# A decoder step on one core: where the recurrence's small products and the square sums stand among the large projections

## The chip, the cores and the metric

The kernel runs on one core of a Trainium2 chip. A core has five engines with their own instruction streams: PE multiplies matrices, DVE, ACT and POOL work on vectors, and SP issues DMA transfers (the others can issue some too). They meet at semaphores. The metric is the device time of one launch in microseconds (us).

## The reference

One inference step of a decoder with two layers of width 1024 in float32. A prompt of 16 + 1024 tokens and eight single sample tokens go through a causal convolution layer, an MLP, an RWKV-7 layer, a second MLP and a final norm. The change lies in the RWKV-7 layer, whose core is this (cut):

```python
r = (xr @ w_r).astype(f32)
k = (xk @ w_k).astype(f32)
v = (xv @ w_v).astype(f32)
w_log = -jax.nn.softplus(-(w0 + jnp.tanh(xw @ w1) @ w2).astype(f32)) - 0.5
decay = jnp.exp(-jnp.exp(w_log))
a = jax.nn.sigmoid((a0 + (xa @ a1) @ a2).astype(f32))
g = jax.nn.sigmoid(xg @ g1) @ g2
...
kk = (k * k_k.astype(f32)).reshape(hs)
kk = kk / jnp.maximum(jnp.sqrt(jnp.sum(kk * kk, axis=-1, keepdims=True)), L2_EPS)
...
def _wkv7_step(S, inp):
    r_t, w_t, k_t, v_t, kk_t, a_t = inp
    sa = jnp.einsum('bhvk,bhk->bhv', S, -kk_t)
    S = (S * w_t[:, :, None, :] + sa[..., None] * (kk_t * a_t)[:, :, None, :]
         + v_t[..., None] * k_t[:, :, None, :])
    y = jnp.einsum('bhvk,bhk->bhv', S, r_t)
    return S, y
```

The three large projections have 1024 x 1024 weights; decay, a and g come through low-rank pairs of weights (64, 64 and 128 wide). The state S has 16 heads of 64 x 64 and runs over the prompt's tokens one after the other.

## The kernel before

Activations lie with the channel on the 128 partitions, in eight blocks of channels (KT = 8), and the tokens along the row.

**Token groups.** The RWKV projections run in four groups of 272, 256, 256 and 264 tokens, called 0 to 3 here as in the code (`mixer_in(g, ...)`, L967); the third group is g == 2. In a group the loop over p (L1108) takes one block of 128 output channels at a time: the projection pr with w_r (eight matmuls, `proj`, L919), perhaps a projection pk with w_k for the *next* group (`keys`, L927; `keys_amid` and `keys_behind` say which, L914), the low-rank products l_g, l_w and l_a (L1120, L1129), the projection pv with w_v (L1133). Then come the products of the block before (`finish`/`trace`, L1054): transposes vt, the small products nn, and the bonus sum (a matmul into a tile that is also called pk, L1101), and last pb, which spreads the norm of kk over its heads (L1141).

**The square sums.** `keys` needs the sum of the squares of k_k * k per head. ACT squares each pk into sq (L948), and four small matmuls add it into pn (L939). They stand one key block late: those of block p follow the projection of block p + 1.

**The recurrence** is computed in 17 chunks of 64 tokens. Its steps for a chunk are small products: A (L1274, on 64 rows), gg and po (L1325, 32 x 32), bT (L1343, full transposes), W (L1350), U (L1366), S (L1377) and Y (L1384, L1386). Between them DVE, ACT and POOL move results out of PSUM: w, uv, fs, sv, xa, nr, sw, no. DVE also inverts 32 x 32 triangles (L1236, L1237, tiles ni and tt), and finished rows are normed (ems, ey, eq on ACT and DVE, yn on PE). SP loads a chunk's operands (xa, bk, p, sv, uv) in between the blocks of weights.

**Ticks.** These steps are pushed into the projections by `tick` (L1584). Each call takes a step of the inversion, gives the recurrence some credit and lets it emit steps until the credit is used up, and takes a step of the norm:

```python
PACE = [0, 1.4, 1.3, 2.4]
...
def tick(g, slow):

    invert()
    advance(PACE[g] * slow, NCH - 1)
    next(ng, None)
```

Group 0 has pace 0, so its ticks emit nothing of the recurrence. A block p has five ticks: one at its start, two inside pr (after the third and the sixth matmul), two inside pv. A key projection has two of its own in groups 1 and 2 at the same two places (when it runs for the next group).

**What sets the order.** In this stage PE's instructions stand in the order in which the program writes them (`tc.manual_schedule(engines={nc.tensor.engine})`, L1590). The order on the other engines is chosen by a scheduler, when the program is built, from a timeline of its own. Results of matmuls go to PSUM: four banks (tag mm) rotate among the projections and low-rank products, three (tag w) among the recurrence's products, one (tag x) holds pn.

Of the kernel before, what the change touches and what calls it, by code (L numbers as in the profile page):

```python
# [8 lines left out]
F32 = mybir.dt.float32  # L9
# [7 lines left out]
P = 128  # L17
# [16 lines left out]
N1 = 272  # L34
# [12 lines left out]
def hybrid_step(tc, x_prompt, x_sample, state_conv, state_shift, state_wkv, meta_tokens,  # L47
# [10 lines left out]
    with ctx:  # L58
# [48 lines left out]
        for name, ap in vecs:  # L107
            n = ap.shape[0]
# [85 lines left out]
        def bank(name, tag="mm"):  # L194
            return cur[tag].tile([P, 512], F32, name=name, tag=tag)
# [200 lines left out]
        with ExitStack() as l0:  # L396
# [294 lines left out]
            with ExitStack() as s:  # L691
# [14 lines left out]
                for g in range(3):  # L706
# [125 lines left out]
        pr = pool(ld, "pr", 1)  # L832
# [85 lines left out]

        def proj(w, act, n, name, fill=None):  # L919
            ps = bank(f"p{name}")  # L920
            for k in range(KT):
                nc.tensor.matmul(ps[:, :n], w[:, k, :], act[k], start=k == 0, stop=k == KT - 1)  # L922
                if fill and k in (2, 5):
                    fill()
            return ps

        def keys(g, fill):  # L927
# [5 lines left out]
            pn = bank(nm("pn"), "x")  # L933
            add_pn = lambda: None

            def to_pn(p, sq):
                def add():
                    for j in range(4):
                        nc.tensor.matmul(pn[32 * j:32 * j + 32, :n // 4], head_sel(p), sq[:, n // 4 * j:n // 4 * (j + 1)],  # L939
                                         start=p == 0, stop=p == KT - 1, tile_position=(0, 32 * j))  # L940
                return add
            for p in range(KT):
                yield
                ps = proj(next(wrkv), act, n, nm("k", p), fill)
                k_ = kept[g, p] = pr.tile([P, N1], F32, name=nm("st", p), tag="st", bufs=KT + 1)
                nc.scalar.copy(k_[:, :n], ps[:, :n])
                sq = pr.tile([P, N1], F32, name=nm("sq", p), tag="rk", bufs=2)
                nc.scalar.activation(sq[:, :n], ps[:, :n], AF.Square, scale=vec("k_k", p))  # L948
                add_pn()
                add_pn = to_pn(p, sq)  # L950
            yield
# [3 lines left out]
            norm[g] = lorap.tile([P, N1], F32R, name=nm("r16"), tag="r16", bufs=2)[:, :n]  # L955
            add_pn()
            nc.vector.tensor_scalar(r16, pn[:, :w], L2_EPS * L2_EPS, None, op0=ALU.max)
# [9 lines left out]
        def mixer_in(g, tick):  # L967
# [63 lines left out]
            def t_(name, p, tag=None, bufs=1):  # L1031
                return pr.tile([P, N1], F32, name=nm(name, p), tag=tag or name, bufs=bufs)
# [8 lines left out]
            dd = lambda p, i, src: nc.gpsimd.tensor_copy(ddec[:, p, i, :], src)  # L1041
            both = lambda: tick(1.0)
            wg, ww = gate_w(), rate_w()
            gate(wg)
# [9 lines left out]
            def finish(p, rk, ab, vv):  # L1054
                def trace():
                    for s in segs:
# [41 lines left out]
                    if g == 0:  # L1098
                        nc.gpsimd.dma_start(d_n[0, p], n32[:, 4])
                    pb = bank(nm("pk", p))  # L1100
                    nc.tensor.matmul(pb[:, :n], hsum, rk[:, :n], start=True, stop=True)  # L1101
# [4 lines left out]

            late, later = (lambda: lambda: None), lambda: None
            for p in range(KT):  # L1108
                both()
                ps = proj(next(wrkv), act, n, nm("r", p), both if p else first)  # L1110
                rk2 = pr.tile([P, 2, N1], F32, name=nm("rk2", p), tag="rk2", bufs=2)
# [23 lines left out]
                nc.scalar.copy(vv[:, :n], ps[:, :n])  # L1135
                later()
                later = late()
                nkk, rp = (rk2[:, i, :] for i in range(2))
# [649 lines left out]
```

## Time and profile before

| | |
|---|---|
| median of three runs | 2652.7 us (2650.81 to 2654.59) |
| profiled execution | 2651.75 us |
| its span, first to last instruction | 2649.8 us |
| mean granted clock of PE | 0.994 |
| groups 0 to 3 of the projections, from about | 1106, 1236, 1396 and 1562 us |
| PE busy in the stretch from 1106 to 1713 us | 582.3 of 607 us |

The span is that of the profiled execution; times inside it are counted from its first instruction. In the rows of the instructions in order of time, a row holds a start, a busy time from the first start to the last end, the engine, the line, and the result and operands of a run of equal instructions; `128*128` is the part of PE's array that a matmul uses (rows times columns). One float32 matmul is recorded as two, so a projection of eight is x16. Behind them in brackets stands the idle time before a row and who ended it. In the rows by stretch, the columns are the stretch, its length, the busy time of each engine with its count of instructions, PE's granted clock, the share of the DMA engines and GB/s.

### The profile page before, as it was taken

The page shows a single profiled execution, that of the slowest core. Times are in us where ns is not written, and L with a number is a line of the kernel's source. Part 1 is how long each engine was busy: PE and PEld are TensorE (multiplying, and loading weights), DVE is VectorE, ACT ScalarE, POOL GpSimd, SP SyncE. Part 2 cuts the span into 40 slices and gives each one's busy share as a digit, 9 for nine tenths or more (in the row PEclk, how much of TensorE's full clock was granted, in tenths as well). Part 3 has the DMA queues.
Part 4 walks back from the last instruction along what each step waited for, and adds up shares of the span by engine and source line. Part 5 has one row for each costly group of instructions (what it writes and reads, how often), then busy time and mean ns, then how long its engine had stood idle before and what let it go on. Part 6 is the DMA issues. An engine that isn't in the chain of part 4 may idle for free.

```text
span 2649.8 us, 51719 instructions
## 1 busy us (share of the span) xinstructions
PE 2594.1 (98%) x19956; PEld 2432.9 (92%) x19956; DVE 1717.6 (65%) x3610; ACT 1128.8 (43%) x2093; POOL 1456.7 (55%) x2060
## 2 busy tenths in 40 slices
PE   9999999999999999999999999899999999999998
PEld 8999999999999999777777777789999999999998
DVE  6999999997444444445757567686679554444435
ACT  5546435444444333243344545545444542222223
POOL 7677878878878777022211113476588763333331
PEclk9999999999999999999999999999999999999999
DMA  7663544554446543677776867898575542222211
GB/s 190 172 168 108 167 141 133 160 172 137 138 138 187 155 136 112 191 211 202 214 184 181 213 160 194 218 207 195 142 219 174 153 132 65 72 68 69 72 48 44
DMA packets 602060, 400.24 MB, mean 151 GB/s; under 512 B 96128, under 2 KB 548928, under 8 KB 601814
## 3 DMA queue, kind: packets, MB, share of 16 engines
q1 hardware_dynamic: 573764, 360.08, 49.6%
q0 software_dynamic: 8720, 26.35, 3.0%
q10 hardware_dynamic: 19330, 10.49, 1.4%
q8 instruction: 158, 2.59, 0.4%
q14 instruction: 88, 0.72, 0.1%
HBM read 338.94 MB, written 58.83 MB: 150 GB/s over the span
## 4 chain that ended last, share of the span: by engine, by line
PE 85%; DVE 8%; ACT 2%; issue 2%; DMA 1%; POOL 1%; SPq 0%; ACTq 0%; DVEq 0%; POOLq 0%
PE ps_in L190 8%; PE ps_in L192 8%; PE ps_in L191 8%; PE out L190 8%; PE out L191 8%; PE out L192 8%; PE pk L922 4%; PE pr L922 4%; PE pv L922 3%; PE ps_g L190 1%; PE ps_o L192 1%; PE ps_g L191 1%; PE ps_g L192 1%; PE ps_oo L190 1%; PE ps_o L190 1%
## 5 line engine op out<-in xcount | busy, mean ns | idle before, releaser
L165 POOL TENSOR_TENSOR wo_lo<-wo_raw,wo_hi 128x256 fp32r<-128x256 f32 x736 | 543.0, 770 | 286.6 <-ACT wo_hi L158 279.2
L165 POOL TENSOR_TENSOR wi_lo<-wi_raw,wi_hi 128x256 fp32r<-128x256 f32 x640 | 474.5, 774 | 238.3 <-ACT wi_hi L158 237.9
L190 PE MATMUL out<-hh,wo_hi 128*128 128x352 f32 (+2 forms) x1536 | 497.5, 324 | 8.1 <-DVE h L360 6.5
L360 DVE TENSOR_TENSOR h<-h,out 128x352 f32<-128x352 f32 (+2 forms) x768 | 386.9, 512 | 168.2 <-PE out L192 166.6
L190 PE MATMUL ps_in<-m_h,wi_hi 128*128 128x352 f32 (+2 forms) x1536 | 494.0, 322 | 0.0
L192 PE MATMUL ps_in<-m_l,wi_hi 128*128 128x352 f32 (+2 forms) x1536 | 492.8, 321 | 0.7 <-DVE m_l L288 0.7
L191 PE MATMUL out<-hh,wo_lo 128*128 128x352 f32 (+2 forms) x1536 | 492.5, 321 | 0.0
L191 PE MATMUL ps_in<-m_h,wi_lo 128*128 128x352 f32 (+2 forms) x1536 | 491.5, 320 | 0.0
L192 PE MATMUL out<-hl,wo_hi 128*128 128x352 f32 (+2 forms) x1536 | 490.8, 320 | 0.0
L542 DVE SCALAR_TENSOR_TENSOR cv<-u,wdw,cv 128x348 f32<-128x348 f32 (+2 forms) x720 | 378.8, 577 | 0.7
L158 ACT CAST wi_hi<-wi_raw 128x1024 fp32r<-128x1024 f32 x160 | 167.6, 1049 | 383.7 <-PE out L192 191.1
L158 ACT CAST wo_hi<-wo_raw 128x1024 fp32r<-128x1024 f32 x184 | 192.7, 1048 | 313.0 <-PE out L192 167.1
L190 PEld LDWEIGHTS out<-hh,wo_hi 128*128 128x128 f32 x1536 | 289.1, 188 | 13.7 <-DVE h L360 9.0
L190 PEld LDWEIGHTS ps_in<-m_h,wi_hi 128*128 128x128 f32 x1536 | 289.2, 188 | 1.4
L192 PEld LDWEIGHTS ps_in<-m_l,wi_hi 128*128 128x128 f32 x1536 | 288.2, 188 | 2.0 <-DVE m_l L288 1.5
L191 PEld LDWEIGHTS out<-hh,wo_lo 128*128 128x128 f32 x1536 | 288.5, 188 | 0.8
L191 PEld LDWEIGHTS ps_in<-m_h,wi_lo 128*128 128x128 f32 x1536 | 288.5, 188 | 0.6
L192 PEld LDWEIGHTS out<-hl,wo_hi 128*128 128x128 f32 x1536 | 288.3, 188 | 0.0
L347 DVE SCALAR_TENSOR_TENSOR ps_in<-ps_in,rs_m 128x352 f32<-128x352 f32 (+2 forms) x192 | 100.7, 525 | 256.5 <-PE ps_in L192 256.1
L142 DVE TENSOR_TENSOR hl<-ps_in,hh 128x352 fp32r<-128x352 f32 (+2 forms) x192 | 98.9, 515 | 124.0 <-ACT hh L141 123.9
L1097 POOL DMA_DIRECT2D d_n<-n x32 | 24.5, 764 | 220.4 <-DVE n L1087 130.8
L348 ACT ACTIVATE ps_in<-ps_in 128x352 f32<-128x352 f32 (+2 forms) x192 | 85.1, 444 | 129.4 <-DVE ps_in L347 129.2
(371 smaller groups left out, 4734.5 us busy)
## 6 DMA issues: line engine op xcount, KB each, us to landing
wi_raw<-in_w_mlp_in_dram SPq DMA_DIRECT2D x160, 512.0 KB
wo_raw<-in_w_mlp_out_dram SPq DMA_DIRECT2D x160, 512.0 KB
wk_raw<-in_rwkv_w_k_dram SPq DMA_DIRECT2D x32, 512.0 KB
wr_raw<-in_rwkv_w_r_dram SPq DMA_DIRECT2D x32, 512.0 KB
wv_raw<-in_rwkv_w_v_dram SPq DMA_DIRECT2D x32, 512.0 KB
d_ab<-ab POOLq DMA_DIRECT2D x32, 512.0 KB, 4.3
pg_raw<-in_conv_w_pw_dram SPq DMA_DIRECT2D x24, 512.0 KB
pa_raw<-in_conv_w_pw_dram SPq DMA_DIRECT2D x24, 512.0 KB
```

The lines of the kernel that those rows point to most:

```text
L142: return eng_lo.tensor_sub(lo, src, hi.bitcast(F32))
L158: cast = nc.scalar.copy(hi[:, :a * b], raw[:, :a * b])
L165: eng_lo.tensor_sub(lo[:, cs], raw[:, cs], hi[:, cs].bitcast(F32))
L190: nc.tensor.matmul(ps, w[0], act[0], start=first, stop=False)
L191: nc.tensor.matmul(ps, w[1], act[0], start=False, stop=False)
L192: nc.tensor.matmul(ps, w[0], act[1], start=False, stop=last)
L347: nc.vector.scalar_tensor_tensor(s, s, 0.0, rs()[:, :n], op0=ALU.max, op1=ALU.mult)
L348: nc.scalar.activation(s, s, AF.Square)
L360: total = nc.vector.tensor_add(hv[:, 4 * i + m, :], hv[:, 4 * i + m, :], ps[:, :n])
L542: nc.vector.scalar_tensor_tensor(acc[m][:, :n], ug[:, m, j:j + n], wdw[:, m, j:j + 1], acc[m][:, :n], op0=ALU.mult, op1=ALU.add)
L922: nc.tensor.matmul(ps[:, :n], w[:, k, :], act[k], start=k == 0, stop=k == KT - 1)
L1097: nc.gpsimd.dma_start(d_n[ch0:ch0 + ncg, p].rearrange("c r t -> r c t"), n32[:, :ncg])
```

## The change

The ticks get other places. In groups 0, 1 and 3 a block still has five, one each: at the block's start (not for p = 0), in the middle of pr, behind l_w and l_a, in the middle of pv, and behind nn. In group 2 there are none in pr and pv (block 0 keeps two in pr, where the last step of the keys hangs on them): three follow each other behind l_w and l_a, and two behind nn. The ticks in the key projections stay.

The square sums are put on a list, `sums`, and emitted behind l_a of the block, each right after its own key projection rather than one later. sq and rk, which share a tag, get three buffers rather than two.

```diff
-        def proj(w, act, n, name, fill=None):
+        def proj(w, act, n, name, fill=None, at=(2, 5)):
             ps = bank(f"p{name}")
             for k in range(KT):
                 nc.tensor.matmul(ps[:, :n], w[:, k, :], act[k], start=k == 0, stop=k == KT - 1)
-                if fill and k in (2, 5):
+                if fill and k in at:
                     fill()
             return ps
+        sums = []
...
-            add_pn = lambda: None
-
...
-                sq = pr.tile([P, N1], F32, name=nm("sq", p), tag="rk", bufs=2)
+                while len(sums) > (p == 1 and g > 0):
+                    sums.pop(0)()
+                sq = pr.tile([P, N1], F32, name=nm("sq", p), tag="rk", bufs=3)
                 nc.scalar.activation(sq[:, :n], ps[:, :n], AF.Square, scale=vec("k_k", p))
-                add_pn()
-                add_pn = to_pn(p, sq)
+                sums.append(to_pn(p, sq))
...
-            add_pn()
+            sums.pop(0)()
...
+            lumps = g == 2
+            spaced = (lambda: None) if lumps else both
...
-                def trace():
+                def trace(fill):
...
+                    for _ in range(1 + lumps):
+                        fill()
                     pb = bank(nm("pk", p))
                     nc.tensor.matmul(pb[:, :n], hsum, rk[:, :n], start=True, stop=True)
...
             for p in range(KT):
-                both()
-                ps = proj(next(wrkv), act, n, nm("r", p), both if p else first)
+                if p:
+                    spaced()
+                ps = proj(next(wrkv), act, n, nm("r", p), *((spaced, (3,)) if p else (first,)))
...
+                while sums:
+                    sums.pop(0)()
+                for _ in range(3 if lumps and p else 1):
+                    both()
...
-                ps = proj(next(wrkv), act_v, n, nm("v", p), both)
+                ps = proj(next(wrkv), act_v, n, nm("v", p), spaced, (3,))
...
-                later = late()
+                later = late(both)
...
-                rk = t_("rk", p, "rk", 2)
+                rk = t_("rk", p, "rk", 3)
...
-                late()()
+                late(lambda: None)()
```

How this moves instructions is seen best in the order of single engines. First PE in block 4 of group 2, before (W, po and U are the recurrence's; the rows left out are matmuls of the same projection):

```order
L922 MATMUL pr_4_16361<-mx_0_5_15378,wr_4_raw 128x256
L1350 MATMUL W_16368<-sv,xa_12365 64x64 x16
L1325 MATMUL po_16390<-p_15917,gg_16280 32x32 x16
L922 MATMUL pr_4_16361<-mx_0_6_15380,wr_4_raw 128x256
...
L922 MATMUL pk_2_16415<-mx_2_7_15838,wk_2_raw 128x264
L939 MATMUL pn_15840<-sq_1_16237,hsel 32x66 x4
L1028 MATMUL l_g_16432<-lg_15328,wg_12353 128x256
L1129 MATMUL l_w_16438<-lwa,wa_12355 128x256
L1129 MATMUL l_a_16439<-lwa,wa_12355 128x256
...
L922 MATMUL pv_4_16448<-mx_3_2_15421,wv_4_raw 128x256
L1366 MATMUL U_16452<-w_16385,p_16283 64x64 x16
L922 MATMUL pv_4_16448<-mx_3_3_15423,wv_4_raw 128x256
```

and now:

```order
L922 MATMUL pk_2_16378<-mx_2_7_15838,wk_2_raw 128x264
L1028 MATMUL l_g_16391<-lg_15328,wg_12353 128x256
L1138 MATMUL l_w_16397<-lwa,wa_12355 128x256
L1138 MATMUL l_a_16398<-lwa,wa_12355 128x256
L938 MATMUL pn_15840<-sq_2_16389,hsel 32x66 x4
L1363 MATMUL W_16405<-sv,xa_12365 64x64 x16
L1338 MATMUL po_16427<-p_15931,gg_16319 32x32 x16
...
L922 MATMUL pv_4_16452<-mx_3_7_15431,wv_4_raw 128x256
L1070 MATMUL vt_3_16465<-ident,vv_3_16272 128x128 x2
L1087 MATMUL nn_3_16472<-ab_3_16360 32x32 x16
L1379 MATMUL U_16491<-w_16422,p_16322 64x64 x16
L1105 MATMUL pk_3_16520<-rk_3_16358,hsum 128x256
```

W, po and pn now follow l_a, pn with the sq of this block's own key (sq_2, not sq_1), U follows nn, and pr, pk and pv are whole.

Then ACT in block 1 of group 2, before (vv is the copy that empties pv; bkt, gg, p, ems are the recurrence's and the norm's):

```order
L1333 COPY gg_15719<-gg_15702 32x256 x2
L1146 ACTIVATE em_1_15793<-wa_1_15681 128x256
L1150 ACTIVATE ex_1_15795<-wa_1_15681 128x4x64
L1344 COPY bkt_15725<-bT_15726 128x512
L1344 COPY bkt_15725<-bT_15732 128x512
L1504 ACT_TABLE_LOAD
L1504 ACTIVATE ems_15645<-ems_15645,eps_t 128x8
L1155 COPY wc<-ex_1_15795 128x4
L1135 COPY vv_1_15756<-pv_1_15692 128x256
```

and now:

```order
L1168 COPY wc<-ex_1_15795 128x4
L1401 COPY ey_15642<-Y_15609 128x512
L1292 COPY no_15308<-A_15652 32x128
L1292 COPY no_15308<-A_15653 32x128
L1513 ACTIVATE eq_15669<-ey_15642 128x512
L1148 COPY vv_1_15701<-pv_1_15692 128x256
L1072 COPY vt_0_15705<-vt_0_15704 128x256
L1073 DMA d_v<-vt_0_15705 128x2x128
L1346 COPY gg_15753<-gg_15736 32x256 x2
L1357 COPY bkt_15759<-bT_15760 128x512
L1357 COPY bkt_15759<-bT_15766 128x512
L1517 ACT_TABLE_LOAD
```

The copy vv has moved ahead of the table load and behind the square eq.

Last ACT in block 4 of group 3, before:

```order
L1154 ACTIVATE ex_4_18554<-wa_4_18492 128x8
L1504 ACT_TABLE_LOAD
L1504 ACTIVATE ems_18478<-ems_18478,eps_t 128x8
L1155 COPY wc<-ex_4_18554 128x4
L1135 COPY vv_4_18514<-pv_4_18503 128x264
```

and now:

```order
L1167 ACTIVATE ex_4_18554<-wa_4_18486 128x8
L1168 COPY wc<-ex_4_18554 128x4
L1148 COPY vv_4_18513<-pv_4_18503 128x264
L1072 COPY vt_3_18518<-vt_3_18517 128x256
L1073 DMA d_v<-vt_3_18518 128x2x128
L1517 ACT_TABLE_LOAD
L1517 ACTIVATE ems_18493<-ems_18493,eps_t 128x8
```

The load and the root behind it have moved from ahead of vv to behind it. Elsewhere the scheduler has moved the readers of the recurrence's products along with them, on DVE and ACT by some rows, on SP (xa, bk, sv, uv, p against the blocks of weights) and POOL (sw, and small copies) by one to five. No matmul is added or taken away, and behind the stage PE's order is the same.

More of the change, by code (lines that the diff above doesn't have):

```diff
@@ L1105, in finish, with none_yet @@
                 return trace
-            late, later = (lambda: lambda: None), lambda: None
+            def none_yet(fill):
+                for _ in range(1 + lumps):
+                    fill()
+                return lambda: None
+            late, later = none_yet, lambda: None
             for p in range(KT):
-                both()
-                ps = proj(next(wrkv), act, n, nm("r", p), both if p else first)
+                if p:
+                    spaced()
+                ps = proj(next(wrkv), act, n, nm("r", p), *((spaced, (3,)) if p else (first,)))
                 rk2 = pr.tile([P, 2, N1], F32, name=nm("rk2", p), tag="rk2", bufs=2)
```

## The prediction

> **What bounds the kernel now.** I read the page first (busy time and the chain that ended last), then the four token groups of the RWKV projections as stretches of time, then the waits of PE in them, and last the instructions in order of time at the places where the change moves something.
>
> ```profile
> PE 2594.1 (98%) x19956; PEld 2432.9 (92%) x19956; DVE 1717.6 (65%) x3610; ACT 1128.8 (43%) x2093; POOL 1456.7 (55%) x2060
> ...
> PE 85%; DVE 8%; ACT 2%; issue 2%; DMA 1%; POOL 1%; SPq 0%; ACTq 0%; DVEq 0%; POOLq 0%
> ```
>
> PE is busy for 98% of the span and holds 85% of the chain, so PE time that is saved shortens the run, unless it turns into a wait. The change touches only the stage of the four groups. Its stretches, one row for each group:
>
> ```profile
> core 0: us, PE busy (x) PEld busy (x) DVE busy (x) ACT busy (x) POOL busy (x), PEclk, DMA share, GB/s
> 1106.00:1236.00 130.00, 128.27 (x870) 100.04 (x869) 59.35 (x150) 49.72 (x144) 31.58 (x59) 1.00 0.64 193
> 1236.00:1396.00 160.00, 155.18 (x1556) 123.67 (x1555) 99.71 (x262) 63.85 (x165) 29.62 (x52) 0.98 0.81 203
> 1396.00:1562.00 166.00, 159.80 (x1823) 127.47 (x1822) 112.62 (x272) 78.26 (x193) 30.17 (x48) 0.99 0.77 202
> 1562.00:1713.00 151.00, 139.01 (x1816) 110.16 (x1810) 101.70 (x233) 78.35 (x195) 46.39 (x92) 0.99 0.71 179
> ```
>
> PE idles for 1.7, 4.8, 6.2 and 12.0 us in groups 0 to 3 (stretch less busy time): 24.7 us that the new order may lose or add to. Busy time is no proof of useful work, though. What the change works on is inside it.
>
> **What a small product costs when it interrupts a large one.** Two neighbouring blocks of group 1, the first with its value projection (pv) whole, the second with a product on half rows (A) in its middle:
>
> ```profile
> 1259.58 3.72 PE L922 MATMUL pv<-mx,wv_raw 128*128 128x256 f32 x16
> 1263.14 0.38 PE L1068 MATMUL vt<-ident,vv 128*128 128x128 f32 x2
> ...
> 1269.10 1.56 PE L922 MATMUL pv<-mx,wv_raw 128*128 128x256 f32 x6
> 1270.59 1.16 PE L1274 MATMUL A<-xa,bk 64*128 64x128 f32 x16
> 1271.68 2.42 PE L922 MATMUL pv<-mx,wv_raw 128*128 128x256 f32 x10
> 1273.95 0.38 PE L1068 MATMUL vt<-ident,vv 128*128 128x128 f32 x2
> ```
>
> Whole, pv takes 1263.14 - 1259.58 = 3.56 us. Interrupted, it takes 4.85 us, of which A holds 1.09, so pv itself has become 3.76: 0.20 us more. That is one emptying of the array before the change of tile shape and one slow start behind it, what one change of shape costs. A pays the like within its own 1.09. Now two small products of unlike shape behind each other, and two of the same:
>
> ```profile
> 1582.16 1.15 PE L1377 MATMUL S<-uv,bkt 128*64 128x64 f32 x32
> 1583.14 1.10 PE L1384 MATMUL Y<-sv,xa 128*64 128x64 f32 x32
> ...
> 1596.87 1.15 PE L1350 MATMUL W<-sv,xa 128*64 128x64 f32 x32
> 1597.95 0.69 PE L1325 MATMUL po<-p,gg 32*32 32x32 f32 x32
> ```
>
> From start to start S takes 0.98 before Y of the same shape, and W, equal in size, 1.08 before po of another. So it is the change of shape that costs, not the step from small to large. Joining two islands of small products removes one change, not two. The Trainium skill, page "TensorEngine Tiling (Array Packing)", section "Tiling Modes", says that a change of the tiling mode, and not one of the tile alone, drains the engine. By that rule the changes of shape are to be counted, and the trace agrees with 1.08 against 0.98; were small after small free, 88 ends of islands (153 islands before, 109 after) would go and the gain be 88 x 0.20 = 17.6 us.
>
> **The change, part by part.** In PE's order I count the changes of tile shape from the first gate product to the last bonus product: 52, 83, 92 and 90 in groups 0 to 3 before; 45, 71, 72 and 79 after. That is 7, 12, 20 and 11 fewer, 50 in all. Every matmul stays, and the recurrence arrives at the same place: from the first product with w_o on, PE's order is the same.
> - The square sums (pn) go beside l_w and l_a in groups 0 to 2. Five of eight join that island (one change less each), one more joins its neighbour whole (two less): 7 a group, 21 x 0.20 = 4.2 us.
> - The ticks account for the other 29: 5 in group 1, 13 in group 2, 11 in group 3: 5.8 us.
>
> Together -10.0 us. Some of it cannot be cashed. At the start of the last two groups DVE runs behind with the 32x32 inverses (L1236, L1237), and PE waits for it:
>
> ```profile
> 1591.30 1.43 PE L1343 MATMUL bT<-ident,bk 128*128 128x128 f32 x8 [3.20 <-DVE nr L1284]
> ...
> 1587.48 1.09 DVE L1237 TENSOR_TENSOR ni<-ni,tt 128x150 f32<-128x150 f32 x1
> 1590.29 0.43 DVE L1282 TENSOR_TENSOR xa<-A,m_ar 64x256 f32<-64x256 f32 x1
> ...
> 1592.00:1596.00 4.00, 4.00 (x13) 3.25 (x14) 3.93 (x11) 1.67 (x3) 3.04 (x4) 0.57 0.98 213
> ```
>
> A PE that comes earlier there only waits longer. About ten of the 31 changes of groups 2 and 3 lie in such blocks: +2.0 us. In block 0 of group 3 the new order puts A directly ahead of pb, gg and bT, where two eights of pv stood between; I leave this wait of 3.20 as it is.
>
> Three other waits lose their cause in the new order of ACT. Each is PE waiting for a bank of PSUM (four rotate) that ACT has not emptied.
>
> ```profile
> 1427.21 0.39 PE L814 MATMUL pb<-r,hspread 128*128 128x256 f32 x1 [2.07 <-ACT vv L1135]
> ...
> 1424.13 1.07 ACT L1344 COPY bkt<-bT 128x512 f32<-128x512 f32 x2
> 1425.20 1.28 ACT L1504 ACT_TABLE_LOAD   x1
> 1426.50 0.30 ACT L1504 ACTIVATE ems<-ems,eps_t 128x8 f32<-128x8 f32 x1
> 1426.79 0.36 ACT L1135 COPY vv<-pv 128x256 f32<-128x256 f32 x1
> ...
> 1425.00:1429.00 4.00, 1.93 (x8) 1.51 (x8) 3.38 (x11) 2.42 (x6) 0.27 (x1) 0.93 1.03 190
> 1429.00:1432.00 3.00, 3.00 (x10) 1.91 (x8) 3.00 (x9) 0.00 (x0) 1.55 (x4) 0.52 0.22 71
> ...
> 1658.24 0.39 PE L814 MATMUL pb<-r,hspread 128*128 128x264 f32 x1 [1.75 <-ACT vv L1135]
> ...
> 1656.23 1.28 ACT L1504 ACT_TABLE_LOAD   x1
> 1657.81 0.37 ACT L1135 COPY vv<-pv 128x264 f32<-128x264 f32 x1
> ...
> 1655.00:1662.00 7.00, 5.25 (x55) 3.98 (x53) 5.33 (x12) 3.43 (x9) 3.65 (x9) 1.00 1.09 309
> ...
> 1463.33 1.56 PE L922 MATMUL pv<-mx,wv_raw 128*128 128x256 f32 x6 [1.26 <-ACT sq L948]
> ...
> 1461.99 0.63 ACT L1500 ACTIVATE eq<-ey 128x512 f32<-128x512 f32 x1 [4.59 <-DVE ey L1498]
> 1462.79 0.49 ACT L948 ACTIVATE sq<-pk,pvec 128x264 f32<-128x264 f32 x1
> ```
>
> In block 1 of group 2 the copy vv stands behind two copies and a table load, and after the wait the granted clock is 0.52 for 3 us, which costs another 1.5. In the new order vv stands ahead of the load there, and in block 4 of group 3 too, and gg and bT (1.5 us) come between pv and pb. In block 3 of group 2 the copy st and the square sq stood behind eq, which waited for DVE; eq now comes later. So 2.07 + 1.5 + 1.75 + 1.26 = 6.6 us may go. But ACT's work has not shrunk; vv of block 1 now stands behind another eq. Nothing lost and all of it gained are the bounds, and I take half: -3.3 us. The Trainium skill, page "TensorE: Matmul & The Clock Gate", section "HAM oscillation", sets the limit of idleness that halves the clock at some 3.4 us. By it the wait of 2.07 would not have cost the 1.5; the rows show 0.52 after 2.07 and 1.00 around 1.75, so here the trace decides.
>
> At nothing I cost: the wait of pn for its own sq. Until now pn took the sq of the key before. Now it follows l_a, as pv did, and pv needed the same sq (its bank is that of the key); the 1.26 above is that wait's longest. The time under it is l_g, l_w and l_a; without ACT being free each pn would add up to 1.26, and all that PE has still to do stands behind it. The SP queue changes the places of xa, bk, sv and uv against the weight blocks by a few rows, POOL those of sw and ddec. Apart from the one below, no wait of PE in the stage ends with a transfer, so I price these at 0, within 0.7 either way.
>
> ```profile
> PE pb L814 <- ACT vv L1135: 10.1, 8, 3.6
> PE p_wa L1003 <- DMA wa_raw<-d_lr: 0.7, 1, 0.7
> ```
>
> Sum: -10.0 + 2.0 - 3.3 = -11.3 us. The profiled execution took 2651.75 us (span 2649.8), 0.95 below the median of the runs shown; 2652.7 - 11.3 = 2641.4.
>
> **The rivals.** A change of 0.2% (5.3 us) is about what a measurement of this kernel tells from none.
> - The waits come back (2649). The three named waits only move on, pn waits 0.2 us in some fifteen places, and DVE holds back 3 us instead of 2: -10.0 + 3 + 3 = -4. For it: vv is the copy that PE waits for most (10.1 us in eight waits, the row above). Against it: in group 2 the ticks now lie between l_a and pv, so ACT gets time.
> - Everything is cashed (2636). All the named waits go and DVE costs nothing: -16.6. For it: group 2 idles 6.2 us, and more than half of it is named above. Against it: DVE is busy for 112.6 of 166 us there.
> - Slower, by lumps that starve PE. Three ticks in a row put S, Y and A, or W and po, behind each other, and their readers on DVE (fs, sv, xa, nr) come in one heap. If bT, A or Y then waits as at 1591.30, each lump costs 3.20 and, with a clock of 0.57 over 4 us, another 1.7: 4.9. Two such waits eat the 10.0; it is slower by over 0.2% from the fourth on: -10.0 + 4 x 4.9 = +9.6, 2662. Against it: pv whole (3.56 us) follows each lump and gives DVE that time.
>
> **How the numbers follow.** Forecast 0.56, everything cashed 0.18, waits that come back 0.16, starving lumps 0.10. The first two are faster by over 0.2%: 0.74; the third is within: 0.16; the fourth slower: 0.10. The forecast's own range is 2637 to 2647. For eight in ten I go from 2634, a little under everything cashed, to 2653, the upper edge of the waits that come back, and leave the slower case and little else out.
>
> **What would show it.** Right: pv or pr of group 2 in one piece of sixteen, 3.56 us long; the PE busy time of groups 0 to 3 lower by some 10 us together; pb of block 1 in group 2 without its 2 us. Group 0, which has no recurrence, should be 7 x 0.20 = 1.4 us shorter whatever else happens. Wrong: more than 25 us of idle PE in the stage, a clock near 0.5 in group 2 at new places, or pn waiting for sq.

## The result and the profile after

The changed kernel takes 2641.17 us in the median of five runs (2639.78 to 2643.76). Beside it, on the same chip, the kernel before took 2654.03 (five runs, 2650.81 to 2657.02): a ratio of 0.9951, interval 0.9941 to 0.9962, or 12.9 us less. The forecast was 2641.4, within 2634 to 2653, a gain of 11.3 us from the 2652.7 that was known then. The total and the term for the shapes came out; the two terms for waits did not come out singly, and that is what the rest of this document is about.

The page of the changed kernel, busy time and chain:

```profile
PE 2584.5 (98%) x19956; PEld 2439.1 (92%) x19956; DVE 1720.5 (65%) x3610; ACT 1129.0 (43%) x2093; POOL 1453.0 (55%) x2060
...
PE 86%; DVE 8%; DMA 2%; ACT 2%; issue 1%; POOL 0%; ACTq 0%; SPq 0%; DVEq 0%; POOLq 0%
```

PE is busy 9.6 us less (2594.1 before) and is still the bound. The number of matmuls is the same, so each now costs less, not fewer are made.

To compare stage by stage, both traces have to be cut at the same instructions. I cut at the first p_g of each token group (the low-rank product that opens it) and, behind group 3, at the first ps_oo (the product with w_o). Rows by stretch, of before:

```profile
1108.10:1232.90 124.80, 123.07 (x847) 95.90 (x839) 56.86 (x145) 48.87 (x143) 31.58 (x59) 1.00 0.64 192
1232.90:1385.40 152.50, 147.68 (x1454) 117.72 (x1446) 97.37 (x256) 59.21 (x157) 28.32 (x50) 0.98 0.82 206
1385.40:1555.70 170.30, 164.10 (x1852) 131.07 (x1848) 114.16 (x276) 80.63 (x198) 30.31 (x48) 0.99 0.76 199
1555.70:1714.60 158.90, 145.31 (x1908) 115.25 (x1900) 104.46 (x241) 82.46 (x204) 47.56 (x93) 0.99 0.72 183
```

and of after:

```profile
1111.40:1235.30 123.90, 121.74 (x848) 96.30 (x840) 57.23 (x145) 48.85 (x143) 31.79 (x59) 1.00 0.68 193
1235.30:1382.70 147.40, 143.67 (x1449) 117.53 (x1445) 96.27 (x256) 58.63 (x157) 28.56 (x50) 0.99 0.84 213
1382.70:1546.50 163.80, 157.37 (x1856) 131.92 (x1848) 113.67 (x275) 81.31 (x198) 29.45 (x48) 1.00 0.78 205
1546.50:1706.00 159.50, 148.56 (x1908) 121.42 (x1900) 105.35 (x242) 82.47 (x204) 46.86 (x94) 0.94 0.72 186
```

Groups 0 to 2 are shorter by about 1, 5 and 6.5 us. Group 3 is not shorter at all: 159.5 against 158.9, and its clock has fallen from 0.99 to 0.94. Read as three terms, cut exactly at those instructions:

| us | length | idle PE | PE busy at half clock | remainder* |
|---|---|---|---|---|
| group 0, before / after | 124.8 / 123.9 | 1.7 / 2.2 | 0 / 0 | 123.1 / 121.7 |
| group 1 | 152.4 / 147.4 | 4.8 / 3.7 | 6.2 / 3.4 | 144.5 / 142.0 |
| group 2 | 170.4 / 163.8 | 6.2 / 6.4 | 3.4 / 0 | 162.5 / 157.4 |
| group 3 | 158.9 / 159.5 | 13.6 / 11.0 | 3.4 / 16.4 | 143.6 / 140.4 |

\* length less idle time less half of the busy time at half clock. Small products at half clock do not quite take double (the four of yn take 1.12 us instead of 0.66, in rows shown further down), so with 16.4 us at half clock group 3's remainder is a little too low.

The remainder is mostly the cost of the products themselves, and it falls by 1.4, 2.5, 5.1 and 3.2. Idle time changes by +0.4, -1.1, +0.2 and -2.6 (26.4 to 23.3 in total); 1.8 of group 3's is the wait of the first ps_oo at its end, which is gone. The extra time at half clock, 19.8 us against 13.0, costs some 3 us.

The remainder also holds a part of each wait. In these traces PE counts as busy until the end of a matmul, but the next one starts before that end where nothing holds it up. The bonus sum (pk) of block 1 of group 2 before, where pb then waits (1427.21, shown in the prediction), and pk and pb of block 2 now, without a wait:

```profile
1424.44 0.70 PE L1101 MATMUL pk<-rk,hsum 128*128 128x256 f32 x2
...
1434.06 0.70 PE L1105 MATMUL pk<-rk,hsum 128*128 128x256 f32 x2
1434.41 0.47 PE L814 MATMUL pb<-r,hspread 128*128 128x256 f32 x1
```

Unhindered, pb starts 0.35 us after pk; the wait's 2.07 us are counted only from 0.70 us after it. So each such wait costs 0.35 us more than its idle time. In the stage pb waits for vv three times now and eight times before (four of them in group 2, now none; two in group 3, now one). About 1.8 us of the remainder's fall are these five waits; some 10 are left for the products.

Together the groups and the block of keys ahead of them take 627.7 us instead of 639.6, 11.9 less. The profiled execution lost 3.3 us before the change begins (its stage starts at 1078.3, before at 1075.0; the eleven other kernels of this study start it at 1074.5 to 1076.5) and gained 1.8 behind it: -11.9 + 3.3 - 1.8 = -10.4, against -10.3 between the spans.

The stage's waits of PE after, by engine and line waited for (total, times, longest):

```profile
PE bT L1356 <- DVE nr L1297: 4.1, 4, 3.3
PE pb L814 <- ACT vv L1148: 3.9, 3, 3.5
PE yn L1559 <- ACT uv L1381: 3.2, 1, 3.2
PE gg L1338 <- ACT em L1159: 3.0, 1, 3.0
PE Y L1397 <- DVE nr L1297: 2.6, 2, 1.6
```

pb's waits for vv have gone from 10.1 us to 3.9. The longest of them, in group 1, is as it was (3.56 us before, 3.49 now). yn and gg, which did not head the list before, are new; gg's wait is put down to ACT's em here and to DVE's nr in most other traces. Two of these waits, followed back, with what they do to the clock (first the instructions, then stretches of 4 us):

```profile
1441.74 0.68 DVE L1380 COPY uv<-U 64x512 f32<-64x512 f32 x1
1442.46 0.58 ACT L1381 COPY uv<-U 64x512 f32<-64x512 f32 x1 [6.17 <-DVE uv L1380]
1443.09 0.66 PE L1559 MATMUL yn<-ident,ey 128*128 128x128 f32 x4 [3.17 <-ACT uv L1381]
...
1578.77 2.32 POOL L1369 TENSOR_TENSOR sw<-sv,wc 64x512 f32<-64x512 f32 x2 [4.60 <-DVE sv L1408]
1579.08 1.09 DVE L1249 TENSOR_TENSOR tt<-ni 128x184 f32<-128x184 f32 x1
...
1583.07 0.42 DVE L1297 TENSOR_TENSOR nr<-A,m_ar 128x256 f32<-128x256 f32 x1
...
1583.54 1.12 PE L1356 MATMUL bT<-ident,bk 128*128 128x128 f32 x4 [3.31 <-DVE nr L1297]
```

```profile
1443.00:1447.00 4.00, 3.91 (x20) 3.50 (x21) 3.85 (x11) 1.32 (x5) 0.75 (x1) 1.00 0.64 190
...
1584.00:1588.00 4.00, 4.00 (x13) 3.18 (x12) 3.90 (x10) 1.12 (x2) 2.31 (x3) 0.50 0.45 102
...
1616.00:1620.00 4.00, 3.89 (x33) 3.47 (x30) 3.45 (x12) 2.10 (x5) 0.41 (x3) 0.50 0.12 31
```

During the waits of yn, bT and gg themselves DVE is busy for 3.17 of 3.17, 3.25 of 3.31 and 2.89 of 3.04 us, and in the stretches behind them for 3.5 to 3.9 of 4 us. Both waits shown end with DVE (ACT's copy of uv waits 6.17 us for DVE's). After the wait of 3.17 in group 2 the clock stays at 1.00; after bT's 3.31 and gg's 3.04 in group 3 it is 0.50.

### The profile page after: what moved, and what is told of

Read it like the earlier page. It is cut to its first block, busy times and chain, and to the rows that moved or that the text cites. A ratio compares the mean times of both kernels' runs of the same rounds, so it can differ in the third digit from the quotient of the medians.

```text
span 2639.5 us, 51709 instructions
## 1 busy us (share of the span) xinstructions
PE 2584.5 (98%) x19956; PEld 2439.1 (92%) x19956; DVE 1720.5 (65%) x3610; ACT 1129.0 (43%) x2093; POOL 1453.0 (55%) x2060
## 4 chain that ended last, share of the span: by engine, by line
PE 86%; DVE 8%; DMA 2%; ACT 2%; issue 1%; POOL 0%; ACTq 0%; SPq 0%; DVEq 0%; POOLq 0%
PE ps_in L190 8%; PE ps_in L192 8%; PE ps_in L191 8%; PE out L190 8%; PE out L191 8%; PE out L192 8%; PE pk L922 4%; PE pr L922 4%; PE pv L922 3%; PE ps_g L190 1%; PE ps_o L192 1%; PE ps_g L191 1%; PE ps_g L192 1%; PE ps_oo L190 1%; PE ps_o L190 1%
## 5 line engine op out<-in xcount | busy, mean ns | idle before, releaser
L190 PEld LDWEIGHTS out<-hh,wo_hi 128*128 128x128 f32 x1536 | 289.1, 188 | 16.4 <-DVE h L360 11.7
L142 DVE TENSOR_TENSOR hl<-ps_in,hh 128x352 fp32r<-128x352 f32 (+2 forms) x192 | 98.9, 515 | 124.0 <-ACT hh L141 123.9
```

The source lines that it names most:

```text
L142: return eng_lo.tensor_sub(lo, src, hi.bitcast(F32))
L190: nc.tensor.matmul(ps, w[0], act[0], start=first, stop=False)
```

## Experiments

Ratios are to the kernel before on the same chip, with 95% intervals; us are medians. "Changes" are changes of tile shape on PE in groups 0 to 3. "Both inverses" are those of chunks 5 to 8 and 9 to 12, the "third inverse" that of chunks 9 to 12.

| kernel | changes | us | ratio |
|---|---|---|---|
| before | 52, 83, 92, 90 | 2654.03 | 1 |
| the change | 45, 71, 72, 79 | 2641.17 | 0.9951 [0.9941, 0.9962] |
| square sums alone | 45, 76, 85, 90 | 2647.21 | 0.9976 [0.9966, 0.9985] |
| ticks alone | 52, 77, 78, 79 | 2645.78 | 0.9969 [0.9958, 0.9981] |
| pn singly | 82, 107, 108, 79 | 2663.21 | 1.0032 [1.0020, 1.0043] |
| even everywhere | 45, 71, 81, 79 | 2642.82 | 0.9961 [0.9949, 0.9974] |
| inverses left out | as the change | 2629.98 | 0.9904 [0.9891, 0.9918] |
| lumps in groups 2 and 3 | 8 fewer than the change | 2651.07 | 0.9986 [0.9977, 0.9996] |
| third inverse faster | 9 more than the change | 2659.65 | 1.0013 [1.0005, 1.0022] |
| third inverse slower | 18 fewer than the change | 2652.36 | 0.9999 [0.9991, 1.0008] |
| both inverses on POOL | as the change | 2646.57 | 0.9969 [0.9960, 0.9979] |
| third inverse on POOL | as the change | 2644.23 | 0.9955 [0.9942, 0.9969] |
| inverses half on POOL | as the change | 2645.47 | 0.9967 [0.9955, 0.9980] |

All edits below are against the changed kernel.

### Each half alone

Square sums alone: the ticks stand where they stood before.

```diff
-            lumps = g == 2
-            spaced = (lambda: None) if lumps else both
...
-                if p:
-                    spaced()
-                ps = proj(next(wrkv), act, n, nm("r", p), *((spaced, (3,)) if p else (first,)))
+                both()
+                ps = proj(next(wrkv), act, n, nm("r", p), both if p else first)
...
-                for _ in range(3 if lumps and p else 1):
-                    both()
...
-                ps = proj(next(wrkv), act_v, n, nm("v", p), spaced, (3,))
+                ps = proj(next(wrkv), act_v, n, nm("v", p), both)
...
-                later = late(both)
+                later = late(lambda: None)
```

> The square sums stand beside l_a as in the changed kernel; the ticks stay where they were before. Changes of tile shape in groups 0 to 3: 45, 76, 85, 90 (before 52, 83, 92, 90), 21 fewer. Theory (each change of shape costs 0.20 us of PE): 4.2 us faster than before, 1.4 of it in each of groups 0 to 2; idle PE as before within 3 us. Rival (the gain is a matter of waits on ACT and DVE, which the ticks' places set): no faster than before by over 1 us.

Ticks alone: the square sums stand behind the next key projection again.

```diff
-                while len(sums) > (p == 1 and g > 0):
-                    sums.pop(0)()
...
+                while sums:
+                    sums.pop(0)()
                 sums.append(to_pn(p, sq))
...
-                while sums:
-                    sums.pop(0)()
```

> The ticks stand as in the changed kernel; the square sums stay one key late, behind the key projection. Changes of shape 52, 77, 78, 79, 31 fewer than before. Theory: 31 x 0.20 = 6.2 us faster by shape, and the waits of pb in block 1 of group 2 and block 4 of group 3 (2.07 and 1.75 us) gone as in the changed kernel: 6 to 10 us faster than before, and slower than the changed kernel by 3 to 5. Rival (waits alone): as fast as the changed kernel within 1.5 us.

Measured against the common before (2653.81), the sums gain 6.6 us (4.2 expected from the shapes) and the ticks 8.0 (6 to 10 expected). Both halves gain, neither needs the other, and 0.24% + 0.31% = 0.55% is about the 0.49% of both. In the trace of the sums alone the remainder, as defined above, falls by 1.4, 1.4, 0.8 and 0 us in the four groups: 3.6 for 21 changes, 0.17 each (0.14 without the 0.7 us of two waits of pb that are gone). In that of the ticks alone it falls by 0, 1.6, 4.1 and 3.2: 8.9, of which six waits of pb hold 2.1, so 6.8 for 31 changes, some 0.2 each. The rest of the gain of the sums alone is 1.1 us less idle time in the stage and half clock for 6.8 instead of 13.0 us, which is partly chance (see the end). With the sums alone, and not with the whole change, pn does wait once for its sq:

```profile
PE pn L938 <- ACT sq L949: 1.4, 1, 1.4
```

### More changes of shape, and nothing else

This kernel makes the same matmuls, but puts the square sums one at a time between the matmuls of pv. It was made to measure the disputed price.

```diff
-                def add():
-                    for j in range(4):
+                def add(js=range(4)):
+                    for j in js:
...
-                while sums:
-                    sums.pop(0)()
+                parts = [lambda s=s, j=j: s([j]) for s in sums for j in range(4)]
+                sums.clear()
...
+                def single():
+                    calls[0] += 1
+                    if calls[0] % 2 and parts:
+                        parts.pop(0)()
+                    if calls[0] == 4:
+                        spaced()
+                calls = [0]
-                ps = proj(next(wrkv), act_v, n, nm("v", p), spaced, (3,))
+                ps = proj(next(wrkv), act_v, n, nm("v", p), single, range(KT))
+                while parts:
+                    parts.pop(0)()
```

> The changed kernel, but the four small products that add one square into pn stand singly between the matmuls of pv, every second one, instead of together behind l_a. The work is the same; the changes of shape are 82, 107, 108, 79: 109 more than in the changed kernel. Theory: 109 x 0.20 = 21.8 us slower than the changed kernel, 7.4 of it in group 0, where no recurrence can blur it. Rival (changes of shape hide behind other work): within 3 us of the changed kernel.

It takes 22.0 us more than the changed kernel (2663.2 - 2641.2; by the ratios 0.81% of 2654, 21.5) for 109 more changes: 0.20 each. The instructions in order of time in group 0, and the row of the whole group 0 (from its p_g to the next):

```profile
1163.52 0.30 PE L938 MATMUL pn<-sq,hsel 128*32 128x64 f32 x2
1163.75 1.18 PE L922 MATMUL pv<-mx,wv_raw 128*128 128x272 f32 x4
1164.86 0.30 PE L938 MATMUL pn<-sq,hsel 128*32 128x64 f32 x2
1165.09 1.18 PE L922 MATMUL pv<-mx,wv_raw 128*128 128x272 f32 x4
```

```profile
1109.60:1239.80 130.20, 129.28 (x844) 96.56 (x840) 57.40 (x145) 48.85 (x143) 31.17 (x59) 1.00 0.65 183
```

Group 0 has 37 more changes and 129.28 us of busy PE against 121.74: 7.5 us, 0.20 each, at full clock and without more idle time. The rival that changes of shape hide behind other work is out.

A part of this 0.20 may not be the change of shape. Together the four of a square stand on different columns of the array (`tile_position=(0, 32 * j)`) and run side by side. Eight matmuls of pn in a row, in the changed kernel:

```profile
1178.70 0.32 PE L938 MATMUL pn<-sq,hsel 128*32 128x64 f32 x8
1178.95 1.41 PE L922 MATMUL pv<-mx,wv_raw 128*128 128x272 f32 x5
```

The eight take 0.25 us to the start of pv; two alone take 0.23 (1163.52 to 1163.75). Sixteen in a row take 0.36 us elsewhere in this trace (1164.71 to 1165.07), so four side by side cost 0.055. If each alone cost as much, the eight would lose 8 x 0.055 - 2 x 0.055 = 0.33 us by standing singly, beside seven more changes of shape. By this estimate 0.05 of the 0.20 is lost company, and some 0.15 us are the change of shape itself.

In this profile the price shows as busy time; a page that counts busy PE does not tell it from work.

### Are the lumps of group 2 worth anything?

```diff
-            lumps = g == 2
+            lumps = False
```

> The changed kernel without lumps: group 2 has its five ticks spread like groups 1 and 3. Changes of shape 45, 71, 81, 79, 9 more than in the changed kernel, all in group 2. Theory: 1.8 us slower by shape; with the waits that a new order of ACT brings in group 2 (6.2 us of idle PE there before) 0 to 5 us slower than the changed kernel. Rival (lumps starve PE and the gain comes from elsewhere): faster than the changed kernel by 2 us or more, with less idle PE in group 2.

2642.8 us, 0.9961 [0.9949, 0.9974]. It has nine more changes in group 2, whose length is 168.8 us instead of 163.8, of which 6.0 us busy at half clock. In the medians the difference to the change is 1.7 us, near the 1.8 that nine changes cost, but the two intervals overlap: that the lumps of group 2 pay is likely and not settled. The rival, faster by 2 us or more without lumps, did not come.

```diff
-            lumps = g == 2
+            lumps = g >= 2
```

> The changed kernel with lumps in group 3 as well. Changes of shape 45, 71, 72, 71: 8 fewer than in the changed kernel, all in group 3. By shape alone 1.6 us faster. But with a pace of 2.4 three ticks in a row hold steps that need each other's results (W, po and U; gg, bT and W). Theory (a lump starves PE where a step's operand comes from DVE or ACT within the lump): each such place costs 1 to 3 us and a halved clock, and the run is 3 to 12 us slower than the changed kernel, with more than 14 us of idle PE in group 3. Rival (shapes decide everywhere): 1 to 2 us faster.

2651.1 us: with eight changes fewer than the change it is some 9 us slower. The longest wait of PE in group 3, and the clock behind it:

```profile
1605.81 1.97 PE L1397 MATMUL Y<-sv,xa 128*64 128x64 f32 x32 [3.67 <-DVE nr L1297]
```

```profile
1602.00:1606.00 4.00, 0.33 (x10) 0.22 (x7) 3.82 (x11) 2.50 (x10) 1.34 (x5) 0.73 0.57 199
1606.00:1610.00 4.00, 4.00 (x67) 3.88 (x66) 3.80 (x9) 0.47 (x1) 0.61 (x2) 0.50 0.16 36
```

Y stands straight behind A and S and needs xa and nr, which DVE makes from A's result; DVE is busy for 3.82 of the 4 us before, and PE does 0.33 us of work in that time, then 4 us at half clock. Group 3 idles for 17.1 us (change: 11.0) and is busy at half clock for 22.4 (16.4). This is the rival of the starving lumps, true in group 3, where the pace is 2.4. In group 2, at 1.3, it shows once (Y, 1.6 us).

### Does DVE hold back the last two groups?

The inverses of chunks 5 to 8 and 9 to 12, which fall at the starts of groups 2 and 3, are not computed; PE's order is the same.

```diff
-                nc.vector.tensor_add(ni[:, :j, j + 1:top], ni[:, :j, j + 1:top], o)
+                if c not in (5, 9):
+                    nc.vector.tensor_add(ni[:, :j, j + 1:top], ni[:, :j, j + 1:top], o)
```

(and the same around the tensor_mul ahead of it.)

> The changed kernel without the multiplications and additions (tt, ni) that invert the 32x32 triangles of the chunks 5 to 8 and 9 to 12 on DVE; these chunks then use the triangles as they were loaded. All else is the same, PE's order too. Theory (what PE still waits for at the start of groups 2 and 3 is DVE, which is behind with the inverses): the waits of yn in group 2 (3.2 us) and of bT, Y and gg in group 3 (0.8, 3.3, 0.9, 3.0) go down to under 3 us together, the halved clock in group 3 (16.4 busy us) to under 7, and the run becomes 8 to 15 us faster than the changed kernel. Rival (the ticks' places make these waits, whoever is behind): within 4 us of the changed kernel.

2630.0 us, 0.9904 [0.9891, 0.9918]: 11 to 12.5 us less than the change, as the theory said. The start of group 3 in the change, and then here:

```profile
1562.00:1620.00 58.00, 49.76 (x623) 41.28 (x622) 46.34 (x119) 26.06 (x67) 12.55 (x25) 0.90 0.46 114
```

```profile
1562.00:1620.00 58.00, 55.01 (x785) 45.39 (x784) 32.13 (x67) 31.88 (x83) 16.09 (x32) 1.00 0.68 168
```

and PE's instructions there without the inverses:

```profile
1577.12 1.20 PE L1358 MATMUL bT<-ident,bk 128*128 128x128 f32 x8 [0.83 <-ACT gg L1348]
...
1605.30 0.69 PE L1340 MATMUL gg<-x,no 32*32 32x32 f32 x32 [1.58 <-DVE nr L1299]
```

DVE is busy for 32 instead of 46 of the 58 us, the clock is 1.00 instead of 0.90, bT's wait of 3.31 is gone, gg's is halved, and in group 2 yn's of 3.17 has gone too. So the inverses on DVE are what PE waits for there. Together the stage idles for 16.6 us instead of 23.3. It also gives the remainder of group 3 without any time at half clock: 140.8 us, 2.8 below before.

### Can the inverse be spread or moved?

If DVE is what is late, another distribution of the inverse of chunks 9 to 12 should pay. Its steps come in pairs (multiply, add), two pairs to a tick; here four, then one:

```diff
-            every = 4 if c == 0 or c + n == NCH else 3 if c == 1 else 2
+            every = 4 if c == 0 or c + n == NCH else 3 if c == 1 else 4 if c == 9 else 2
```

> The changed kernel, with the inverses of the chunks 9 to 12 given out four pairs of operations a tick rather than two, so that they end in half the ticks. Changes of shape 45, 71, 72, 88, 9 more, since the recurrence then stalls less in group 3. Theory (DVE behind with the inverses is what PE waits for): the waits of group 3's first blocks grow; 1 to 6 us slower than the changed kernel, 1.8 of it by shape. Rival (the waits come from the recurrence's own readers): no slower than 2 us.

```diff
-            every = 4 if c == 0 or c + n == NCH else 3 if c == 1 else 2
+            every = 4 if c == 0 or c + n == NCH else 3 if c == 1 else 1 if c == 9 else 2
```

> The changed kernel, with the same inverses given out one pair a tick rather than two. Changes of shape 45, 71, 72, 61 in the groups, 18 fewer, because a part of the recurrence moves behind them into the products with w_o and the MLP, where it costs its changes as well. Theory: DVE is less crowded in group 3's first blocks, the waits of bT, Y and gg and the halved clock shrink there; 2 to 8 us faster than the changed kernel unless the recurrence that is left over makes new waits later. Rival: within 2 us of the changed kernel.

Faster steps: 2659.7 us, some 16 to 18 us slower than the change; the direction was expected, the size was not. The recurrence comes ready sooner, so more of it moves into group 3 (172.4 us long), and the stage behind loses 20.4 us to idle PE where it lost 11.1. Slower steps: 2652.4 us, about 11 us slower, where 2 to 8 faster was expected. Waits of PE in the whole run with slower steps:

```profile
PE ps_oo L192 <- DVE z_l L142: 6.8, 2, 4.3
PE bT L1356 <- DVE nr L1297: 6.3, 5, 3.3
...
PE ps_in L192 <- DVE m_l L288: 3.8, 2, 3.2
PE gg L1338 <- DVE nr L1297: 3.7, 2, 3.0
```

The waits that were to shrink are the same size (bT 3.3, gg 3.0). What was not done in group 3 is done at its end, in front of ps_oo and ps_in: group 3 shrinks to 142.0 us and the work behind it grows by 28.8. The expectation missed that the pairs set when the recurrence may go on, not only how full DVE is.

Next, POOL does the inverse:

```diff
+            eng = nc.gpsimd if c in (5, 9) else nc.vector
...
-                    nc.vector.tensor_mul(o, ...
-                nc.vector.tensor_add(ni[:, :j, j + 1:top], ni[:, :j, j + 1:top], o)
+                    eng.tensor_mul(o, ...
+                eng.tensor_add(ni[:, :j, j + 1:top], ni[:, :j, j + 1:top], o)
```

> The changed kernel with the inverses of the chunks 5 to 8 and 9 to 12 computed on POOL instead of DVE; nothing else changes, PE's order neither. Theory (PE waits for a DVE that is behind with them, and POOL has the time: it is busy for 20 to 30% of groups 2 and 3): the waits of yn, bT and Y that went when the inverses were left out go here too, and the run is 3 to 9 us faster than the changed kernel. Rival (the inverse only moves: POOL takes longer for each, and POOL at work slows DVE, as the 1.09 us of a tt beside sw against 0.35 hints): the recurrence waits for its triangles, and the run is as slow as the changed kernel or slower by up to 15 us.

The same with `c == 9` alone, which leaves chunks 5 to 8 on DVE:

> The same for the chunks 9 to 12 alone, those of group 3. Theory: the waits of bT, Y and gg in group 3's first blocks shrink by 3 us or more and the halved clock there with them; 2 to 7 us faster than the changed kernel. Rival: as for both groups, no faster than 1 us.

And with every second pair of both on POOL (`c in (5, 9) and j % 2`):

> The same for the chunks 5 to 12, but with every second step of the inverse (multiplication and addition) on POOL and the rest on DVE. Each step needs the one before, so DVE now waits for POOL inside the inverse. Theory (DVE's work in these blocks is what counts): between the changed kernel and the one with both inverses on POOL. Rival (waits on DVE's queue count, since whatever stands behind a waiting step waits too): slower than the changed kernel by 3 us or more.

None beats the change: 2646.6, 2644.2 and 2645.5 us. The gains that the theories named (3 to 9 and 2 to 7 us) did not come. The first is some 5 us slower than the change, as its rival allowed; the second can't be told from it; the third is likely some 4 us slower, which the intervals do not settle. In the second, two waits of PE in the stage, and then a step of the inverse on each engine (durations min/median/max in ns):

```profile
PE gg L1339 <- DVE nr L1298: 8.2, 1, 8.2
...
PE bT L1357 <- DVE nr L1298: 1.3, 4, 0.4
```

```profile
L1250 DVE TENSOR_TENSOR tt<-ni x104: 138/362/832, 1252.7 to 1747.0; 128x30 f32<-128x30 f32 x6, 128x58 f32<-128x58 f32 x6, 128x84 f32<-128x84 f32 x6, 128x108 f32<-128x108 f32 x6
...
L1250 POOL TENSOR_TENSOR tt<-ni x30: 237/567/950, 1560.8 to 1603.8; 128x30 f32<-128x30 f32 x2, 128x58 f32<-128x58 f32 x2, 128x84 f32<-128x84 f32 x2, 128x108 f32<-128x108 f32 x2
```

bT's wait falls from 3.3 to 0.4, as DVE has time (busy for 30.7 of the 58 us, 46.3 in the change); but the inverse, a chain in which each step needs the last, now takes 567 ns a step instead of 362, and gg, which needs its end, waits 8.2 us instead of 3.0. In the first kernel pb in group 2 waits 7.2 us as well, from 1429.47 on. DVE is busy for all but 0.03 of that time, for 4.84 us of it with inputs of the next group (mx) in a row, and only then comes to n, for which pb waits by the profile:

```profile
1429.42 4.84 DVE L887 SCALAR_TENSOR_TENSOR mx<-xx,pvec,hx 128x264 f32<-128x264 f32 x8
```

So there the order on DVE decides; why it differs was not followed. In the third each handover costs (DVE waits 14.5 us for POOL in the inverse). The inverse is bound by its length as a chain as well as by DVE's load.

## Why the prediction came out, step by step

- **The price of a change of shape, 0.20 us: right in size.** Group 0 was to be 1.4 us shorter by seven changes. Its products are (123.1 to 121.7); 0.4 of that went to idle time, so the group is 1.0 shorter. The kernel with pn singly gives 0.20 over 109 changes, or an estimated 0.15 without what pn loses by standing alone. pv of group 2 is whole again, 1477.10 - 1473.54 = 3.56 us as foretold:

```profile
1473.54 3.72 PE L922 MATMUL pv<-mx,wv_raw 128*128 128x256 f32 x16
1477.10 0.38 PE L1070 MATMUL vt<-ident,vv 128*128 128x128 f32 x2
```

- **The shape term, -10.0: right.** The remainder fell by 1.4, 2.5 and 5.1 in groups 0 to 2, and by 2.8 in group 3 if it is taken where no half clock blurs it: 11.8 us. Of this the five waits of pb that are gone hold about 1.8. That leaves 10.0 us for 50 changes: 0.20 a change, and 0.20, 0.21, 0.19 and 0.22 in the four groups. The two kinds are less alike: 0.14 to 0.17 for the square sums alone, some 0.2 for the ticks alone; why was not measured apart.
- **+2.0 for a DVE that is late with the inverses: the mechanism is shown, the size is not.** Taking those inverses away frees 11 to 12.5 us, so DVE holds PE back there as said, in the change by about 7 us of idle time and the rest by the clock. How much of the gain this ate can't be read off: bT's wait in group 3 was left at 3.20 and is 3.31.
- **-3.3 for half of three named waits: wrong as a term.** All three went, not half: pb of block 1 in group 2 follows bT and pk at once, pb of block 4 in group 3 waits 0.23 instead of 1.75, pv no longer waits for sq. But waits of the same size came at places that the prediction did not name: yn 3.17, gg 3.04, Y 1.63. The stage's idle time fell by 3.1 us, 1.8 of it at a place that the prediction did not name (ps_oo at the end of group 3), the ends of pk in front of pb's waits gave another 1.8, and time at half clock rose by 6.8 us. The rival of the waits that come back had the mechanism of the new waits, but not the size.
- **pn waiting for its sq, priced 0: right** for the change (no such wait of over 0.2 us). It can happen: 1.4 us once with the sums alone, 0.7 once with even ticks everywhere.
- **Starving lumps, 0.10: right to keep them small for group 2**, one wait of 1.6 us there; with lumps in group 3 as well they decide.
- **The foretold signs**: PE's busy time in the four groups fell by 8.8 us (580.2 to 571.3) where some 10 were said; time at half clock counts in it. Idle time of the stage stayed under 25 us (23.3); a clock of 0.5 at new places did come, though in group 3 and not in group 2. That is what took the gain of group 3: its remainder is about 3 us lower, its idle time is 2.6 less, and 13 more us at half clock gave it back. This is not one chance execution: with the ticks alone, pn singly and even ticks everywhere group 3 has 11 to 14 us busy at half clock, before and with the sums alone 3.4.

So -11.3 met -11.9 in the stage because the shape term had its size, and because the rest came near in sum: +2.0 - 3.3 = -1.3 was forecast, and -3.1 of idle time, -1.8 in front of waits and some +3 of half clock came. That these nearly agree is luck, since most of the waits that went and all of the half clock behind the new ones were not in the sum.

## What to carry to other kernels

Count the changes of tile shape in PE's order, price one from the trace where a small product cuts a large one, and join the small products; that gain is real even though the profile books its cost as busy time. Where small products are joined, the engine that reads them must have the time: the same lump paid or did no harm at a pace of 1.3 a tick and cost 9 us at 2.4. A fall of PE's busy time is not all shape, either: 0.35 us of each wait of pb stood in it. When the order changes, named waits vanish and others of the same size appear as long as the late engine (here DVE with a serial inverse) is as late as before, so the sum of the waits is better forecast from that engine's load than wait by wait.

## What the runs showed of the hardware that was not expected

**The clock after the same wait.** yn's wait of 3.17 us in group 2 occurs at the same place in seven of these kernels. In the change the clock stayed at 1.00 behind it (1443 to 1447 above). With the ticks alone it did not:

```profile
1443.27 1.12 PE L1557 MATMUL yn<-ident,ey 128*128 128x128 f32 x4 [3.17 <-ACT uv L1379]
```

```profile
1440.00:1444.00 4.00, 0.82 (x6) 0.73 (x5) 4.00 (x10) 1.09 (x3) 0.86 (x2) 0.75 0.09 33
1444.00:1448.00 4.00, 4.00 (x11) 3.22 (x10) 3.78 (x12) 0.76 (x2) 0.00 (x0) 0.50 0.85 253
```

Behind this wait five kernels ran at half clock for about 6.8 us and two at full clock. So a wait of about 3 us has no fixed price. Group 2, in the same order on PE, is 163.8 us long in the change and 166.4 to 166.8 in four of the kernels with half clock there: the wait costs itself, or itself and 2.6 to 3 us more. The clock can also fall within a wait: over bT's 3.31 us it is 0.65 on average. The Trainium skill, page "TensorE: Matmul & The Clock Gate", section "What's actually happening", says that activity is watched in windows of 3.4 us which run freely and do not start with the kernel; the halved stretches in the clock records of this stage, most of them 3.4 or 6.8 us long, agree, and so does the dependence on chance. For a forecast it means that the clock is a term with a spread of its own, several us wide in this stage.

**DVE beside POOL.** In the rows of bT's wait above, a multiply of the inverse (tt, 128x184) takes 1.09 us while POOL computes sw; elsewhere the same shape takes a third of that:

```profile
1611.16 0.34 DVE L1249 TENSOR_TENSOR tt<-ni 128x184 f32<-128x184 f32 x1
```

The 0.75 us are of the same order as what is left of one sw when tt begins, 0.85 us (two take 2.32 together, 1.16 each; tt began 0.31 after the first). The Trainium skill, page "SBUF — State Buffer", section "Who interferes with whom", says that a DVE instruction with two inputs in SBUF contends with a POOL instruction that reads SBUF, and that the port pair they share is an exclusive lock. By that rule tt would take 1.16 - 0.31 + 0.34 = 1.19 us, and the trace's 1.09 agrees about. The 0.75 us are a quarter of bT's wait in size, if it lies on the path to it, which was not tried; and it was in the trace before as well (the 1.09 of ni that the prediction quotes).
